# The first sixty microseconds of a Griffin-style block: all of x requested early, the v products ordered by kind, the squares a block later, the forget chain cut in two

## The chip, the cores and the metric

The kernel runs on 1 core of one Trainium2 chip. The metric is device microseconds of one execution. Before the change it is 734.27 us, the median of 3 runs (734.26 to 735.1).

## What is computed

One layer on x of 512 tokens by 1024 channels, batch 1, all in float32:

```python
h = rms_norm(x, norm_mix_g)
cb, cc, cin, q, k, v, f_logit, g_logit = split(h @ w_in)
u = causal_dwconv(cc * cin, conv_mix_w)                 # three taps
y_conv = (cb * u) @ w_out_conv
log_f = log_sigmoid(f_logit + b_f)                      # 8 heads
F = cumsum(log_f)
s = q.k / 8 + F[t] - F[s]   for s <= t                  # 64 channels a head
y_attn = (softmax(s) @ v) @ w_out_attn
g_conv, g_attn = split(sigmoid(g_logit + b_gate))
x = x + (g_conv * y_conv + g_attn * y_attn) @ w_o
h = rms_norm(x, norm_ffn_g)
a, b = split(causal_dwconv(h @ w_up, conv_ffn_w))
x = x + (silu(a) * b) @ w_down
return rms_norm(x, norm_f_g)
```

## The kernel before

Tokens lie along the free dimension, and channels on the partitions, so x is eight tiles `xs0` to `xs7` of 128 x 512. To keep float32 accuracy on the matmul unit, each operand is split into a high and a low part (`xgh`, `xgl` for x times the gain; `wh`, `wl` for a weight), and each product is three matmuls: high by high, low weight by high x, high weight by low x. The factor of the first RMS norm does not depend on the channel, so it is applied after the products.

**Weights.** All weights come through one stream in the order of the list `stream`: eight chunks `v0` to `v7` (one per block of 128 input channels, 520 columns: 512 of v and 8 forget logits), then the q/k chunks `in12`, `in16`, `in13`, `in17`, then the rest. A chunk is fetched into one of four `raw` buffers (`load`, L135, on SyncE's queue, the first on ScalarE's). `split` (L137 to L153) makes `wh` from it on ScalarE (L151; the first on VectorE, L149) and `wl` on VectorE (L152), each with two buffers. So a fetch waits for the `wl` of four chunks before, and a `wh` waits for the matmuls of two chunks before.

**The v stage** (L243 to L296). A loop over the eight blocks `kb`. Block `kb` asks for x two blocks ahead (`load_x`, L248), splits the weight chunk, makes `xgh` (ScalarE, L264) and `xgl` (VectorE, L266), squares x (ScalarE, L273 and L276) and has GpSimd add the square into `ssq` (L277). Then it issues 24 matmuls: for each of four token tiles `t`, each of the three kinds, a product into `pa[t]` (L281: half of v and the forget logits) and one into `pb[t]` (L282: the other half). In block 0 the kinds are the outer loop. In block 7, after token tile 0, `rstd_col` (L183 to L197) multiplies `ssq` by a column of ones into `pc_n` (L189): TensorE waits there for the last addition. VectorE then makes `ms_n`, and GpSimd raises it to the power -0.5 (`rc_n`, L196), which everything behind it needs.

**q, k and the forget gate** (L507 to L530). TensorE projects q0, k0, q1, k1 (`proj`; 48 matmuls each with the chunks `in12`, `in16`, `in13`, `in17`). Between q0 and k0 the forget logits are transposed into `pz`. `forget` (L478 to L494) makes -log(1+exp(-|z|)) on ScalarE (with two table loads), scans it on VectorE (L489), splits the sum into a high part `fh` (ScalarE, L491) and a low one, and writes both to `fr` (L492 to L494). GpSimd's queue copies rows of `fr` into the operands `qb` and `kb` of the scores (L334). `evac_qk` (L336 to L359) scales a projection on VectorE (`t_q`, `t_k`), and writes its high and low parts on ScalarE, GpSimd and VectorE. The accumulator bank of q1 is that of the next projection, `in4` (`p_in`), which may start only when `t_q` of q1 has read it. Attention follows: each unit of scores (L410, L411) lies between halves of further projections.

**What sets the order.** A scheduler places instructions on each engine by their dependencies; `keep` pins an instruction to the written order, and `after_split` puts what is issued under it behind the latest weight split. Each engine works through its own list in order. GpSimd also clears parts of `qb` and `kb` (twelve memsets, L328 to L330), which the scheduler puts between the additions.

Of the kernel before, what the change touches and what calls it, by code (L numbers as in the profile page):

```python
# [24 lines left out]
AHEAD = 3  # L25
NWARM = 8
NPP = 4
# [6 lines left out]
ME, MO = 185, 186  # L34
# [8 lines left out]
def block_kernel(ctx, tc, xT, vecs, wv, win, wmix, wo, wup, wdn, outT):  # L43
# [10 lines left out]
    def keep(ins):  # L54
        return tc.keep_in_program_order(ins)
# [15 lines left out]
    nc.sync.dma_start(vec, vecs)  # L71

    def col(i):
        return vec[:, i : i + 1]
# [56 lines left out]
    def load(upto):  # L131
        for k in range(len(raws), min(upto, len(stream) - 1) + 1):
            nm, src, ncol = stream[k]
            raw = wp.tile([P, RC], F32, tag="raw", name=f"raw_{nm}", bufs=AHEAD + 1)[:, :ncol]
            keep((nc.scalar if k == 0 else nc.sync).dma_start(raw, src))  # L135
            raws.append(raw)

    def split(hl=None):

        k = len(parts)  # L140
        if k == len(stream):
            return
        nm, _, ncol = stream[k]
        load(k + AHEAD)
        hi, lo = hl or [
            wp.tile([P, WC], F32R, tag=f"w{x}", name=f"w{x}_{nm}", bufs=2)[:, WOFF[x] : WOFF[x] + ncol] for x in "hl"
        ]
        if k == 0:
            keep(nc.vector.tensor_copy(hi, raws[k]))  # L149
        else:  # L150
            order["hi"] = nc.scalar.activation(hi, raws[k], AF.Copy).ins  # L151
        order["lo"] = nc.vector.tensor_sub(lo, raws[k], hi.bitcast(F32)).ins  # L152
# [75 lines left out]
    def ct(name):  # L228
        return ap.tile([P, S], F32, tag="ct", name=name, bufs=NCT)
# [22 lines left out]
    load_x(0, halves[0])  # L252
    load(0)
    load_x(0, halves[1])
    load_x(1)
    load(1)
    for kb in range(KB):
        if kb + 2 < KB:
            load_x(kb + 2)
        wh, wl = chunk(f"v{kb}")  # L260
        x = xs[kb]
        cuts = halves if kb == 0 else [slice(0, S)]
        for cs in cuts:
            nc.scalar.activation(xgh[:, kb, cs], x[:, cs], AF.Copy, scale=col(G1 + kb))  # L264
        for cs in cuts:
            ins = nc.vector.scalar_tensor_tensor(  # L266
                xgl[:, kb, cs], x[:, cs], col(G1 + kb), xgh.bitcast(F32)[:, kb, cs],
                op0=ALU.mult, op1=ALU.subtract,
            )
            if kb == 0:  # L270
                keep(ins)
        if kb == 0:
            nc.scalar.activation(ssq, x, AF.Square)  # L273
        else:
            sq = ap.tile([P, S], F32, tag="pp", name=f"sq{kb}", bufs=NPP)
            nc.scalar.activation(sq, x, AF.Square)  # L276
            nc.gpsimd.tensor_add(ssq, ssq, sq)  # L277

        def vmm(t, x, w, start, stop):
            xt = x[:, kb, t * P : (t + 1) * P]  # L280
            keep(nc.tensor.matmul(pa[t][:, :VW], xt, w[:, :VW], start=start, stop=stop))  # L281
            keep(nc.tensor.matmul(  # L282
                pb[t], xt, w[:, VW:], start=start and t % 2 == 0, stop=stop and t % 2 == 1
            ))

        trio = ((xgh, wh), (xgh, wl), (xgl, wh))
        if kb == 0:
# [175 lines left out]
    def run_all(fs):  # L463
        for f in fs:
            f()
# [8 lines left out]
    for t in range(NT):  # L474
        src = pa[t][:, 4 * HD : VW].unsqueeze(1).to_broadcast([P, 4, H])
        nc.vector.tensor_scalar_mul(zn[:, t], src, rc1[:, t : t + 1])

    def forget():  # L478
        n = 4 * H
        bf, me, mo = vec[:n, BF : BF + 1], vec[:n, ME : ME + 1], vec[:n, MO : MO + 1]  # L480
        z, e, o = ct("fz")[:n, :], ct("fe")[:n, :], ct("fo")[:n, :]
# [3 lines left out]
        nc.scalar.activation(tbl, e[:, :1], AF.Exp)  # L485
# [3 lines left out]
        nc.vector.tensor_tensor_scan(e, o, z, 0.0, op0=ALU.mult, op1=ALU.add)  # L489
        hi = ap.tile([n, S], F32R, tag="ct", name="fh", bufs=NCT)  # L490
# [3 lines left out]
        nc.vector.scalar_tensor_tensor(fr, hi.bitcast(F32), me, e, op0=ALU.mult, op1=ALU.add)  # L494
# [347 lines left out]
```

## Time and profile before

| | |
|---|---|
| median of 3 runs | 734.27 us |
| the profiled execution | 734.09 us |
| its span | 732.3 us |
| TensorE (matmul) busy | 717.3 us, 98% of the span |
| VectorE busy | 400.5 us, 55% |
| ScalarE busy | 292.7 us, 40% |
| GpSimd busy | 140.6 us, 19% |
| mean granted TensorE clock | 0.992 |

A row of the timeline has: start, duration, engine, line, operation, what it writes and reads, the shapes, how many, and in brackets how long the engine had been idle before it and what released it. A row with x2 stands for two instructions that follow one another. A row of the windows has: the stretch, its length, then busy time and number of instructions of TensorE (PE), its weight load (PEld), VectorE (DVE), ScalarE (ACT) and GpSimd (POOL), then the granted clock, the busy share of the DMA engines, and GB/s. A row of the waits has: who waited, for whom, the total, how many times, and the longest.

### The profile page before, as it was taken

How to read it: one execution, taken by the hardware profiler on the slowest of the kernel's cores; microseconds unless marked ns; L12 is line 12 of the kernel's file. 1: busy time of each engine (PE TensorE's matmuls, PEld its weight loads, DVE VectorE, ACT ScalarE, POOL GpSimd, SP SyncE). 2: the span in 40 equal slices, each digit the busy share in tenths (PEclk: the TensorE clock that was granted, in tenths of full speed). 3: DMA queues.
4: the chain of work that ended last, by engine and by line, in shares of the span. 5: the costliest groups of instructions: out<-in, count | busy, mean ns of one | idle time of the engine just before them, and what ended most of it. 6: DMA issues, size and time to landing. Idle time of an engine off the chain costs nothing.

```text
span 732.3 us, 14449 instructions
## 1 busy us (share of the span) xinstructions
PE 717.3 (98%) x6220; PEld 715.0 (98%) x6220; DVE 400.5 (55%) x582; ACT 292.7 (40%) x447; POOL 140.6 (19%) x158
## 2 busy tenths in 40 slices
PE   8989999999999999999999999999999999999995
PEld 7889999999999999999999999999999999999995
DVE  6477666765445445454456666666666673223323
ACT  6374545544433332333344344343353442222321
POOL 6515434322001000113311011101101100000100
PEclk9999999999999999999999999999999999999998
DMA  6523222221222332533313332332322423333303
GB/s 211 162 68 104 77 83 60 59 86 58 88 87 87 90 112 88 166 112 129 114 59 116 94 108 87 106 98 87 115 88 87 115 80 102 88 100 100 110 1 115
DMA packets 23296, 71.39 MB, mean 97 GB/s; under 512 B 2976, under 2 KB 5408, under 8 KB 23232
## 3 DMA queue, kind: packets, MB, share of 16 engines
q1 hardware_dynamic: 20848, 66.98, 29.7%
q0 software_dynamic: 1152, 2.17, 1.0%
q10 hardware_dynamic: 1232, 1.32, 0.6%
q8 instruction: 49, 0.80, 0.5%
q14 instruction: 15, 0.12, 0.1%
HBM read 68.29 MB, written 2.10 MB: 96 GB/s over the span
## 4 chain that ended last, share of the span: by engine, by line
PE 92%; DVE 2%; DMA 2%; ACT 1%; issue 1%; SPq 0%; POOLq 0%; POOL 0%; DVEq 0%; ACTq 0%
PE p_up L174 33%; PE pd L174 14%; PE p_in L174 14%; PE p_wo L174 6%; PE p_gb L174 5%; PE p_ga L174 5%; PE yc L174 3%; PE ya L174 3%; PE o L174 2%; DMA xs<-in_xT_dram 2%; PE tp L439 1%; PE pdA L174 1%; PE p_k L174 1%; PE s L410 1%; PE s L411 1%
## 5 line engine op out<-in xcount | busy, mean ns | idle before, releaser
L174 PE MATMUL p_up<-x1h,wh_up 128*128 128x256 f32 x704 | 137.3, 276 | 0.0
L174 PE MATMUL p_up<-x1l,wh_up 128*128 128x256 f32 x704 | 137.1, 276 | 0.0
L174 PE MATMUL p_up<-x1h,wl_up 128*128 128x256 f32 x704 | 137.0, 276 | 0.0
L174 PEld LDWEIGHTS p_up<-x1h,wh_up 128*128 128x128 f32 x704 | 106.1, 188 | 0.0
L174 PEld LDWEIGHTS p_up<-x1l,wh_up 128*128 128x128 f32 x704 | 106.0, 188 | 0.0
L174 PEld LDWEIGHTS p_up<-x1h,wl_up 128*128 128x128 f32 x704 | 105.9, 188 | 0.0
L690 POOL TENSOR_TENSOR fu<-fu,fu 128x512 f32<-128x512 f32 x22 | 28.4, 1293 | 211.2 <-DVE fu L368 198.3
L152 DVE TENSOR_TENSOR wl_in<-raw_in,wh_in 128x1024 fp32r<-128x1024 f32 x36 | 50.3, 1398 | 30.9 <-ACT wh_in L151 30.4
L152 DVE TENSOR_TENSOR wl_up<-raw_up,wh_up 128x1024 fp32r<-128x1024 f32 x44 | 53.7, 1220 | 14.5 <-ACT wh_up L151 14.5
L174 PE MATMUL pd<-gl,wh_dn 128*128 128x256 f32 x308 | 60.1, 276 | 0.0
L174 PE MATMUL pd<-gh,wh_dn 128*128 128x256 f32 x308 | 59.9, 276 | 0.0
L174 PE MATMUL pd<-gh,wl_dn 128*128 128x256 f32 x308 | 59.9, 276 | 0.0
L174 PE MATMUL p_in<-xgh,wh_in 128*128 128x256 f32 x288 | 56.8, 279 | 0.0
L174 PE MATMUL p_in<-xgl,wh_in 128*128 128x256 f32 x288 | 56.4, 277 | 0.0
L174 PE MATMUL p_in<-xgh,wl_in 128*128 128x256 f32 x288 | 56.4, 277 | 0.0
L152 DVE TENSOR_TENSOR wl_dn<-raw_dn,wh_dn 128x1024 fp32r<-128x1024 f32 (+1 forms) x23 | 26.0, 1132 | 54.9 <-ACT wh_dn L151 54.8
L151 ACT ACTIVATE wh_up<-raw_up 128x1024 fp32r<-128x1024 f32 x44 | 46.4, 1055 | 22.3 <-issue 13.4
L151 ACT ACTIVATE wh_in<-raw_in 128x1024 fp32r<-128x1024 f32 x36 | 38.2, 1061 | 42.5 <-PE ya L174 12.7
L151 ACT ACTIVATE wh_dn<-raw_dn 128x1024 fp32r<-128x1024 f32 (+1 forms) x23 | 22.7, 985 | 66.5 <-PE pd L174 66.2
L174 PEld LDWEIGHTS pd<-gl,wh_dn 128*128 128x128 f32 x308 | 46.5, 188 | 0.0
L174 PEld LDWEIGHTS pd<-gh,wh_dn 128*128 128x128 f32 x308 | 46.3, 188 | 0.0
L174 PEld LDWEIGHTS pd<-gh,wl_dn 128*128 128x128 f32 x308 | 46.3, 188 | 0.0
(223 smaller groups left out, 1611.7 us busy)
## 6 DMA issues: line engine op xcount, KB each, us to landing
raw_up<-in_wup_dram SPq DMA_DIRECT2D x44, 512.0 KB, 3.5
raw_in<-in_win_dram SPq DMA_DIRECT2D x36, 512.0 KB, 3.5
raw_dn<-in_wdn_dram SPq DMA_DIRECT2D x16, 512.0 KB, 3.5
raw_mix<-in_wmix_dram SPq DMA_DIRECT2D x8, 512.0 KB, 3.6
raw_wo<-in_wo_dram SPq DMA_DIRECT2D x8, 512.0 KB, 3.9
raw_dn<-in_wdn_dram SPq DMA_DIRECT2D x8, 384.0 KB, 3.3
xr<-in_xT_dram POOLq DMA_DIRECT2D x8, 256.0 KB, 3.8
raw_v<-in_wv_dram SPq DMA_DIRECT2D x7, 260.0 KB, 4.9
```

The source lines that it names most:

```text
L151: order["hi"] = nc.scalar.activation(hi, raws[k], AF.Copy).ins
L152: order["lo"] = nc.vector.tensor_sub(lo, raws[k], hi.bitcast(F32)).ins
L174: keep(nc.tensor.matmul(out[:, cs], w, x[:, cs], start=start and i == 0 and c == 0, stop=stop and i == 2 and c == len(cut) - 1,))
L410: keep(nc.tensor.matmul(s[:, :nn], QT[pr][:, e, qs], KA[pr][:, e, :nn], start=True, stop=False))
L411: keep(nc.tensor.matmul(s[:, :nn], QB[pr % 2][: KR[e], e, qs], KBt[pr % 2][: KR[e], e, :nn], start=False, stop=True))
L439: keep(nc.tensor.transpose(tp[:, ks], pt[:, ks], ident))
L690: nc.gpsimd.tensor_mul(a, a, b)
```

## The change

1. `load_x` for all blocks is issued ahead of the loop, blocks 0 to 3 in turn with their weight chunks, then blocks 4 to 7 together. The table `vecs` is fetched in two parts: columns 0 to 39 first, the other 147 behind all of x.
2. In blocks 0 to 6 the three kinds of v product are the outer loop, and the token tiles the inner one. Block 7 keeps the tiles outside.
3. The square of block `kb` is made in iteration `kb + 1`; the additions of the first squares are written only when the third is there.
4. In block 1 `xgh` is made ahead of the weight split. Splits and parts of x are pinned in the written order.
5. `forget` ends with the scan. What makes `fr` is a function of its own, `forget_rows`, written behind the projection of k0, and so behind the split of the fourth q/k chunk, `in17`; the evacuations of q0 and k0 follow it. The tiles `fz`, `fe`, `fo` use the `pp` buffers in place of `ct`.

```diff
-    load_x(1)
-    load(1)
+    for kb in range(1, AHEAD + 1):
+        load_x(kb)
+        load(kb)
+    for kb in range(AHEAD + 1, KB):
+        load_x(kb)
+    keep(nc.sync.dma_start(vec[:, CM:], vecs[:, CM:]))
+
+    def square_x(kb):
...
+        sq = ap.tile([P, S], F32, tag="pp", name=f"sq{kb}", bufs=NPP)
+        keep(nc.scalar.activation(sq, xs[kb], AF.Square))
+        sqs.append(sq)
+
+        while kb > 2 and sqs:
+            nc.gpsimd.tensor_add(ssq, ssq, sqs.pop(0))
...
     for kb in range(KB):
-        if kb + 2 < KB:
-            load_x(kb + 2)
...
+        if kb:
+            square_x(kb - 1)
+        if kb == KB - 1:
+            square_x(kb)
...
-        if kb == 0:
+        if kb < KB - 1:
             for i, (x, w) in enumerate(trio):
                 for t in range(NT):
-                    vmm(t, x, w, i == 0, False)
+                    vmm(t, x, w, kb == 0 and i == 0, False)
...
     with after_split():
         forget()
+    run_all(proj(16, "k0", st.append, ring(6)))
+    with after_split():
+        forget_rows()
         evac_qk(0, True)(st[0])
-    run_all(proj(16, "k0", evac_qk(0, False), ring(6)))
+        evac_qk(0, False)(st[1])
```

GpSimd's list before, from the first addition into `ssq` to the power that needs the sum (the numbers behind the names tell buffers apart; `sq1` to `sq7` are the squares):

```order
L277 TENSOR_TENSOR ssq1_108<-ssq1_108,sq4_281 128x512
L328 MEMSET qb1_424 4x512
L277 TENSOR_TENSOR ssq1_108<-ssq1_108,sq5_317 128x512
L329 MEMSET qb1_424 64x512
L328 MEMSET kb0_425 4x512
L277 TENSOR_TENSOR ssq1_108<-ssq1_108,sq6_352 128x512
```

GpSimd's list in the changed kernel, the end of the same stretch, where the additions stand one behind another:

```order
L355 MEMSET kb1_427 4x512
L277 TENSOR_TENSOR ssq1_108<-ssq1_108,sq3_278 128x512
L277 TENSOR_TENSOR ssq1_108<-ssq1_108,sq4_315 128x512
L277 TENSOR_TENSOR ssq1_108<-ssq1_108,sq5_350 128x512
L277 TENSOR_TENSOR ssq1_108<-ssq1_108,sq6_385 128x512
L277 TENSOR_TENSOR ssq1_108<-ssq1_108,sq7_388 128x512
L202 TENSOR_TENSOR rc_n1_404<-ms_n1_402,ex_89 128x4
```

Before, one to five memsets stood between two additions. Now eleven of the twelve memsets stand between the first and the third addition, and the last five additions follow one another.

ScalarE's list before, the end of the v stage (`wh_v` the high weights, `xgh` the high x, `sq` the squares):

```order
L151 ACTIVATE wh_v4_275<-raw_v4_163 128x520
L264 ACTIVATE xgh_95<-xs6_271,vec_64 128x512
L276 ACTIVATE sq7_387<-xs6_271 128x512
L151 ACTIVATE wh_v5_311<-raw_v5_200 128x520
L151 ACTIVATE wh_v6_346<-raw_v6_236 128x520
L151 ACTIVATE wh_v7_381<-raw_v7_273 128x520
```

ScalarE's list in the changed kernel, the same place:

```order
L151 ACTIVATE wh_v6_344<-raw_v6_236 128x520
L286 ACTIVATE xgh_95<-xs6_133,vec_64 128x512
L273 ACTIVATE sq5_350<-xs4_130 128x512
L151 ACTIVATE wh_v7_379<-raw_v7_270 128x520
L286 ACTIVATE xgh_95<-xs6_133,vec_64 128x512
L273 ACTIVATE sq6_385<-xs6_133 128x512
L273 ACTIVATE sq7_388<-xs6_133 128x512
```

The last square stood ahead of the high weights of blocks 5, 6 and 7, and now the last two stand behind those of block 7.

VectorE's list before, from the scan of the forget gate to the scaling of q1:

```order
L489 SCALAR_TENSOR_TENSOR fe_557<-fo_558,fz_556 32x512
L341 SCALAR_TENSOR_TENSOR t_q0_572<-p_q0_489,rb_n1_519 128x512
L492 TENSOR_TENSOR fe_557<-fe_557,fh_567 32x512
L493 TENSOR_SCALAR fe_557<-fe_557,vec_64 32x512
L354 TENSOR_TENSOR a_q0_574<-t_q0_572,a_q0_574 64x512
L494 SCALAR_TENSOR_TENSOR fr_451<-fh_567,vec_64,fe_557 32x512
L354 TENSOR_TENSOR a_q0_574<-t_q0_572,a_q0_574 64x512
L152 TENSOR_TENSOR wl_in17_635<-raw_in17_439,wh_in17_634 128x1024
L343 TENSOR_TENSOR t_k0_638<-p_k0_583,rb_n1_519 128x512
```

VectorE's list in the changed kernel, the same place:

```order
L515 SCALAR_TENSOR_TENSOR fe_459<-fo_460,fz_458 32x512
L155 TENSOR_TENSOR wl_in17_620<-raw_in17_440,wh_in17_619 128x1024
L520 TENSOR_TENSOR fe_459<-fe_459,fh_623 32x512
L366 SCALAR_TENSOR_TENSOR t_q0_628<-p_q0_493,rb_n1_523 128x512
L521 TENSOR_SCALAR fe_459<-fe_459,vec_64 32x512
L368 TENSOR_TENSOR t_k0_639<-p_k0_568,rb_n1_523 128x512
L522 SCALAR_TENSOR_TENSOR fr_452<-fh_623,vec_64,fe_459 32x512
L379 TENSOR_TENSOR a_q0_630<-t_q0_628,a_q0_630 64x512 x2
L379 TENSOR_TENSOR kb0_426<-t_k0_639,a_k0_641 64x512 x2
L155 TENSOR_TENSOR wl_in4_702<-raw_in4_446,wh_in4_701 128x1024
L366 SCALAR_TENSOR_TENSOR t_q1_705<-p_q1_650,rb_n1_523 128x512
```

The low weights of `in17`, which stood behind six instructions after the scan, now stand right behind the scan. Those six, and the scaling and splitting of k0, now stand behind them and ahead of `in4` and of the scaling of q1.

More of the change, by code (lines that the diff above doesn't have):

```diff
@@ L70, in block_kernel @@
     vec = cp.tile([P, NV], F32, tag="vec", name="vec")
-    nc.sync.dma_start(vec, vecs)
+    nc.sync.dma_start(vec[:, :CM], vecs[:, :CM])
     def col(i):
@@ L150, in split @@
         else:
-            order["hi"] = nc.scalar.activation(hi, raws[k], AF.Copy).ins
-        order["lo"] = nc.vector.tensor_sub(lo, raws[k], hi.bitcast(F32)).ins
+            ins = nc.scalar.activation(hi, raws[k], AF.Copy)
+            order["hi"] = ins.ins
+            if k < KB:
+                keep(ins)
+        ins = nc.vector.tensor_sub(lo, raws[k], hi.bitcast(F32))
+        order["lo"] = ins.ins
+        if k < KB:
+            keep(ins)
         parts.append((hi, lo))
@@ L254, in block_kernel, with x_hi @@
     load_x(0, halves[1])
[L255 to L256 removed]
+    for kb in range(1, AHEAD + 1):
[5 more added lines that the diff above has]
+    def square_x(kb):
+        if kb == 0:
+            keep(nc.scalar.activation(ssq, xs[kb], AF.Square))
+            return
+        sq = ap.tile([P, S], F32, tag="pp", name=f"sq{kb}", bufs=NPP)
[3 more added lines that the diff above has]
+            nc.gpsimd.tensor_add(ssq, ssq, sqs.pop(0))
+    sqs = []
     for kb in range(KB):
[L258 to L260 removed]
         x = xs[kb]
         cuts = halves if kb == 0 else [slice(0, S)]
+        def x_hi():
+            for cs in cuts:
+                keep(nc.scalar.activation(xgh[:, kb, cs], x[:, cs], AF.Copy, scale=col(G1 + kb)))
+        if kb == 1:
+            x_hi()
+        wh, wl = chunk(f"v{kb}")
+        if kb != 1:
+            x_hi()
         for cs in cuts:
[L264 to L266 removed]
+            keep(nc.vector.scalar_tensor_tensor(
                 xgl[:, kb, cs], x[:, cs], col(G1 + kb), xgh.bitcast(F32)[:, kb, cs],
                 op0=ALU.mult, op1=ALU.subtract,
[L269 to L277 removed]
+            ))
+        if kb:
+            square_x(kb - 1)
+        if kb == KB - 1:
+            square_x(kb)
         def vmm(t, x, w, start, stop):
@@ L476, in block_kernel @@
         nc.vector.tensor_scalar_mul(zn[:, t], src, rc1[:, t : t + 1])
+    n = 4 * H
+    bf, me, mo = vec[:n, BF : BF + 1], vec[:n, ME : ME + 1], vec[:n, MO : MO + 1]
+    z, e, o = (ap.tile([n, S], F32, tag="pp", name=nm, bufs=NPP) for nm in ("fz", "fe", "fo"))
     def forget():
-        n = 4 * H
-        bf, me, mo = vec[:n, BF : BF + 1], vec[:n, ME : ME + 1], vec[:n, MO : MO + 1]
-        z, e, o = ct("fz")[:n, :], ct("fe")[:n, :], ct("fo")[:n, :]
         nc.scalar.activation(e, pz[:n, :], AF.Abs, bias=bf)
@@ L489, in forget, with forget_rows @@
         nc.vector.tensor_tensor_scan(e, o, z, 0.0, op0=ALU.mult, op1=ALU.add)
+    def forget_rows():
         hi = ap.tile([n, S], F32R, tag="ct", name="fh", bufs=NCT)
```

1 line of the change is left out of this document (removed).

## The prediction

> **What bounds the kernel now.** I read the page first, then TensorE's waits, then the windows, then the timelines of single engines.
>
> ```profile
> PE 717.3 (98%) x6220; PEld 715.0 (98%) x6220; DVE 400.5 (55%) x582; ACT 292.7 (40%) x447; POOL 140.6 (19%) x158
> ```
>
> TensorE is busy for 98% of the span. Only 15 us are left to win by waits, and some of those lie at the two ends. The waits of the first 65 us:
>
> ```profile
> PE pa L281 <- DVE wl_v L152: 2.6, 2, 1.7
> PE p_k L174 <- DVE wl_in L152: 2.5, 1, 2.5
> ```
>
> The windows show what a wait costs beyond itself, and where there is nothing to win:
>
> ```profile
> 7.31:10.72 3.41, 1.79 (x12) 1.17 (x10) 2.11 (x3) 3.04 (x6) 2.39 (x3) 1.00 0.98 363
> 10.72:14.13 3.41, 3.41 (x16) 3.41 (x17) 3.41 (x3) 2.49 (x4) 3.41 (x5) 0.53 0.58 180
> 24.37:27.78 3.41, 2.27 (x18) 2.27 (x19) 1.70 (x2) 0.00 (x0) 0.99 (x2) 1.00 0.35 88
> 51.67:55.09 3.42, 1.41 (x13) 1.21 (x11) 3.29 (x5) 0.74 (x1) 1.34 (x4) 1.00 0.00 0
> 55.09:58.50 3.41, 2.97 (x14) 2.97 (x15) 2.66 (x4) 2.32 (x3) 3.19 (x5) 0.53 0.58 153
> 62.00:75.00 13.00, 13.00 (x114) 13.00 (x113) 8.25 (x19) 5.62 (x13) 3.97 (x7) 1.00 0.32 102
> 197.00:360.00 163.00, 163.00 (x1440) 163.00 (x1439) 77.22 (x84) 56.96 (x69) 25.54 (x22) 1.00 0.35 110
> ```
>
> Where TensorE was busy for 1.79 or 1.41 us of 3.41, the granted clock of the next 3.41 us is 0.53; after 2.27 us it stays at 1.00. From 62 us on TensorE doesn't pause. So the time won at 62 us is the time won in all, and two instants carry the sum: `pc_n` (31.86) and the first matmul of `in4` (62.60).
>
> ```profile
> 16.64 0.28 PE L281 MATMUL pa<-wh_v,xgl 128*128 128x264 f32 x1
> ...
> 23.48 0.28 PE L282 MATMUL pb<-wh_v,xgh 128*128 128x256 f32 x1
> ...
> 31.86 0.95 PE L189 MATMUL pc_n<-ones,ssq 128*128 128x1 f32 x8
> ...
> 47.25 0.39 PE L174 MATMUL p_q<-xgh,wh_in 128*128 128x256 f32 x2
> ...
> 52.69 0.39 PE L174 MATMUL p_k<-xgh,wh_in 128*128 128x256 f32 x2
> 55.53 0.80 PE L174 MATMUL p_k<-xgh,wl_in 128*128 128x256 f32 x2 [2.45 <-DVE wl_in L152]
> ...
> 62.60 0.29 PE L174 MATMUL p_in<-xgh,wh_in 128*128 128x256 f32 x1
> ```
>
> Between 16.64 and 23.48 lie 57 steps: 0.12 us a matmul, so 2.88 us a block of 24. A projection at full pace takes 52.69 - 47.25 = 5.44 us. From the start of k1 to `in4`, with two matmuls of scores between, it took 62.60 - 52.69 = 9.91 in place of 5.44 + 0.24, so 4.23 us are lost there. Of these, 1.6 are the halved clock: 23 pairs from 55.53 on need 5.2 us at full pace, and took 62.36 - 55.53 = 6.8.
>
> **Part 1: x early, order by kind.** ScalarE's rows, in the order of time:
>
> ```profile
> 6.81 0.73 ACT L264 ACTIVATE xgh<-xs,vec 128x512 fp32r<-128x512 f32 x1 [1.02 <-DMA xs<-in_xT_dram]
> ...
> 7.96 0.62 ACT L151 ACTIVATE wh_v<-raw_v 128x520 fp32r<-128x520 f32 x1
> ...
> 9.88 0.62 ACT L151 ACTIVATE wh_v<-raw_v 128x520 fp32r<-128x520 f32 x1
> ...
> 14.91 0.64 ACT L151 ACTIVATE wh_v<-raw_v 128x520 fp32r<-128x520 f32 x1 [1.58 <-PE pb L282]
> ...
> 16.07 0.62 ACT L276 ACTIVATE sq<-xs 128x512 f32<-128x512 f32 x1
> ...
> 21.26 0.72 ACT L264 ACTIVATE xgh<-xs,vec 128x512 fp32r<-128x512 f32 x1 [2.01 <-DMA xs<-in_xT_dram]
> ...
> 47.91 0.20 ACT L485 ACTIVATE tbl<-fe 32x1 f32<-32x1 f32 x1
> ...
> 51.34 1.06 ACT L151 ACTIVATE wh_in<-raw_in 128x1024 fp32r<-128x1024 f32 x1
> ```
>
> The last x tile, asked for behind a waiting weight fetch, held ScalarE for 2.01 us up to 21.26. With all of x asked for at the start that goes. In block 1 the square no longer stands between `xgh` and `wh_v`: `wh_v` can start at 7.5, when `xgh` is done, if its data is there, and no later than the 7.96 of before. I take 7.5, and block 1 at 8.1 (bounds 8.1 to 8.6). Ordering by kind lets `wl_v` come 8 matmuls (0.96 us) after the block's start, and `xgl` 16 (1.92 us). TensorE alone then reaches block 7 at 8.1 + 6 x 2.88 = 25.4, and `pc_n` six matmuls later, at 26.1: 5.8 us early, with no halved clock at 10.72. The SyncE queue pays for it: four x tiles and the rest of `vecs`, 1.1 MB, stand ahead of the fourth chunk onward. At the 363 GB/s of the first window that is 3 us. The chunks of blocks 4 to 7 then land about 14 to 16 us, and block 4 starts at 16.7, so I cost it at nothing; a rival takes it up.
>
> **Part 2: the squares later.** This gives part of it back. VectorE's and GpSimd's rows:
>
> ```profile
> 22.02 0.75 DVE L266 SCALAR_TENSOR_TENSOR xgl<-xs,vec,xgh 128x512 fp32r<-128x512 f32 x1 [2.03 <-ACT xgh L264]
> ...
> 23.07 2.39 DVE L152 TENSOR_TENSOR wl_v<-raw_v,wh_v 128x520 fp32r<-128x520 f32 x1 [0.29 <-ACT wh_v L151]
> ...
> 48.20 1.21 DVE L489 TENSOR_TENSOR_SCAN fe<-fo,fz 32x512 f32<-32x512 f32 x1 [0.89 <-ACT tbl L485]
> 49.34 0.65 DVE L341 SCALAR_TENSOR_TENSOR t_q<-p_q,rb_n 128x512 f32<-128x512 f32 x1
> ...
> 54.25 1.23 DVE L152 TENSOR_TENSOR wl_in<-raw_in,wh_in 128x1024 fp32r<-128x1024 f32 x1
> ...
> 56.78 1.71 DVE L354 TENSOR_TENSOR kb<-t_k,a_k 64x512 fp32r<-64x512 f32 x2 [0.70 <-ACT a_k L352]
> ```
>
> ```profile
> L277 POOL TENSOR_TENSOR ssq<-ssq,sq 128x512 f32<-128x512 f32 x7 | 9.9, 1418 | 5.6 <-ACT sq L276 5.4
> ```
>
> ```profile
> 23.15 0.52 POOL L329 MEMSET kb<- 64x512 f32 x1
> 23.64 1.25 POOL L277 TENSOR_TENSOR ssq<-ssq,sq 128x512 f32<-128x512 f32 x1
> ...
> 53.81 1.27 POOL L334 DMA_DIRECT2D qb<-fr  x2 [2.08 <-DVE fr L494]
> ...
> 56.19 1.76 POOL L353 TENSOR_SCALAR a_k<-t_k 64x512 fp32r<-64x512 f32 x2
> ```
>
> An addition takes 1.25 us when free. One beside the `wl_v` at 23.07 stretched that from about 0.7 to 2.39: the two exclude one another. The `xgl` at 22.02 took its 0.75 us beside memsets, so these cost GpSimd's own time only.
>
> Now the sum. `wh_v` of block 2 starts between 8.5 (behind `wh_v` of block 1 and a square) and the 9.88 of before, say 9.2; the first square ends 1.16 + 0.62 later (14.91 to 16.07, and its own length), at 11.0. GpSimd does the first addition to 12.4, five memsets at 0.52 to 15.0, the second behind a `wl_v` from 15.5 to 16.7, six memsets to 19.8. Then five additions are left, and the two-input instructions of blocks 6 and 7 come in turn with them: 5 x 1.25 + 2 x (0.69 + 0.75) = 9.1, so `ssq` is there at 28.8 in place of the 26.1 where TensorE wants it. Lower bound: the last squares follow `wh_v` of block 7, which follows block 5's end (22.5), so they end at 24.9, and the last addition at 26.9. Upper bound, with each addition at the 1.42 of the group row: 30.0. I take 28.8; `pc_n` comes 31.86 - 28.8 = 3.1 us early.
>
> TensorE would be idle for about 2.7 of the 3.4 us from 25.4 to 28.8: less busy than the two windows that were followed by 0.53. So I expect a halved clock behind it. It cost 1.6 us at k1; part of it falls into the wait, and I take 1.2 (bounds 0 and 1.6).
>
> **Part 3: the forget chain split.** From `pc_n` on, the power, the evacuations and the chain follow as before, so I keep the clock of before. `wh_in` of `in17` goes behind the table of 47.91, to 49.17, `wl_in` behind the scan at 49.34 to 50.6; TensorE wants it at 52.9. The loss of 4.23 goes. What is late next: behind `wl_in` VectorE has five instructions at about 0.7 (as `t_q`), two pairs at 1.71, `wl_in` of `in4` at 1.23 and `t_q` of q1 at 0.65: 50.6 + 3.5 + 3.4 + 1.2 + 0.65 = 59.3, less 0.8, since each starts some 0.07 before the record of the one ahead ends (the scan's ends at 49.41, and `t_q` starts at 49.34): 58.5. That `t_q` frees the bank of `in4`, which TensorE wants at 52.69 + 5.44 + 0.24 = 58.37. A wait of 0.1 to 0.9, say 0.4. The score before it wants `kb`: GpSimd has `qb` and `a_k` (1.76 a pair) behind `t_k`, to 55.4, then the copies.
>
> ```profile
> DMA to landing us min/median/max: 1.6/2.5/3.7
> ```
>
> The first copy into `kb` starts at 55.4 + 1.27 = 56.7 and lands at 58.3 if it takes 1.6, and 60.4 at 3.7; no weight fetch runs beside it, so I take 1.6, inside the 0.4. After that the projections of attention give VectorE time to catch up (8.25 of 13 us busy after 62 before).
>
> From `pc_n` to `in4`: before 30.74. Now 30.74 - 4.23 + 0.4 = 26.9 without the halved clock; with it TensorE comes 1.2 later, the 0.4 is covered, 27.7.
>
> **Sum.** 28.8 + 27.7 = 56.5 against 62.60: 6.1 us. The profiled execution took 734.09 (0.18 below the median), so 728.0.
>
> **Rivals.**
>
> *The sum is in time.* If additions get ahead of VectorE, `pc_n` is at 26.9, no clock falls, and `in4` starts at 26.9 + 26.9 = 53.8: 8.8 us, 725.3. For it: the group's 1.42 contains waits that may shrink. Against: GpSimd has at least 6.2 us of additions left at 19.8, beside VectorE's 2.9. Chance 0.18.
>
> *The clock stays.* [...] Chance 0.20.
>
> *The weights come late.* If the chunks of blocks 4 and on move at the 180 GB/s of the second window, 1.1 MB takes 6 us, block 4 waits some 2.3 us, and the end moves by as much: 730.3. Against: the busiest window had 363. Chance 0.14.
>
> *The fourth weights are still late*, from a wait on ScalarE or its fetch that I don't see. Then only part 1 is won: 3.1 us, 731.0. Chance 0.07.
>
> *Slower: GpSimd and VectorE take turns throughout*, memsets too. The `wl_v` at 23.07 was held 0.57 us before the addition's record began, beside a memset. Then from 11.0 on all is one row: 7 x 1.25 + 11 x 0.52 + 12 x 0.7 = 22.9, `pc_n` at 33.9, two halved windows of 1.6, and `in4` at 33.9 + 26.9 + 3.2 = 64.0: 735.5 at least. It decides from `pc_n` at about 33 on. Against: the 0.75 us `xgl` beside memsets. [...] Chance 0.04.
>
> **How the numbers follow.** My case has 0.37, and its bounds reach from 26.9 + 26.6 to 30.0 + 28.1 for `in4`, which is 725.0 to 729.6. The range reaches from the first rival's 725.3 to the late weights' 730.3, with 0.1 and 0.2 of margin, 725.2 to 730.5; outside are the last two rivals, 0.11, and a tail. A measurement can tell about 0.2%, 1.5 us. All cases but the last are faster, 0.96; half of the third rival's chance I give to no change, since late weights may join it, and a quarter of the slower one: faster 0.93, same 0.04, slower 0.03.
>
> **What would show it.** Right: blocks 1 to 6 without a wait over 0.3 us; a wait of TensorE on `ssq` or on `xgl` of block 7 of about 2.7 us, `pc_n` near 28.8, a granted clock near 0.5 behind it; no wait at k1, a short one at the first score or at `in4`. Wrong: a wait in blocks 4 to 7 for a fetch; `pc_n` before 27 or after 30; a wait on `wl_in` at k1; pauses of TensorE in attention, which would give time back.

## The result, and the profile after

The changed kernel takes 728.13 us, the median of 4 runs (727.26 to 728.9), beside 734.26 us for the kernel before in the same comparison (4 runs, 734.08 to 735.1). The ratio is 0.9914, 95% interval 0.9897 to 0.9931. The forecast was 728.0, in a range of 725.2 to 730.5.

The kernel before is less steady than those four runs suggest. Beside the experiments below it ran 66 times more: 65 of these lie between 729.36 and 735.56 us, with a median near 732.2 (one run of 746.5, at a mean clock of 0.942, is left aside). The changed kernel stayed at 727.3 to 728.9 in 11 runs. In the later comparison the ratio is 0.9941 (0.992 to 0.9962). So the gain is 6.1 us against the runs that the forecast started from, and about 4 against an ordinary one.

The profiled execution after took 728.21 us, with a span of 726.4. The busy time on the page, and TensorE's waits in the first 65 us:

```profile
PE 716.0 (99%) x6220; PEld 714.3 (98%) x6220; DVE 396.9 (55%) x582; ACT 293.0 (40%) x447; POOL 140.9 (19%) x158
```

```profile
PE pc_n L195 <- POOL ssq L277: 1.5, 1, 1.5
...
PE pa L306 <- ACT xgh L286: 0.2, 1, 0.2
```

(The row left out is the wait of the first `ones`, ahead of the v stage, in both kernels.) The waits for `wl_v` in the v stage and for `wl_in` at k1 are gone. One new wait is there, for the sum of squares. TensorE's rows at the two instants that carried the sum, and between them two rows at the ends of the stretch at half pace:

```profile
28.20 1.05 PE L195 MATMUL pc_n<-ones,ssq 128*128 128x1 f32 x8 [1.51 <-POOL ssq L277]
...
29.92 0.34 PE L306 MATMUL pa<-wh_v,xgh 128*128 128x264 f32 x1
...
33.30 0.47 PE L180 MATMUL p_q<-xgl,wh_in 128*128 128x256 f32 x2
...
56.09 0.28 PE L435 MATMUL s<-a_k,a_q 128*128 128x256 f32 x1
56.21 0.30 PE L436 MATMUL s<-kb,qb 68*128 68x256 f32 x1
56.37 0.47 PE L180 MATMUL p_in<-xgh,wh_in 128*128 128x256 f32 x2
```

`pc_n` starts at 28.20 (31.86 before, 28.8 forecast), and `in4` at 56.37 (62.60 before, 56.5 forecast). That is 6.23 us. The span is shorter by 5.9: 0.3 to 0.4 is given back at the very end, where the last matmuls ran at a lower clock this time (0.58 granted in the 1.2 us around them, against 1.00 before). The first row is of the kernel before, the second of the changed one:

```profile
725.55 0.71 PE L203 MATMUL pb_n<-ident,rc_n 128*128 128x128 f32 x4 [1.02 <-POOL rc_n L196]
```

```profile
719.34 1.11 PE L209 MATMUL pb_n<-ident,rc_n 128*128 128x128 f32 x4 [1.03 <-POOL rc_n L202]
```

The windows of the changed kernel around the wait:

```profile
26.50:29.90 3.40, 1.89 (x16) 1.70 (x15) 0.61 (x2) 0.57 (x1) 1.94 (x3) 1.00 0.42 145
29.90:33.30 3.40, 3.40 (x19) 3.40 (x18) 2.09 (x8) 1.48 (x4) 2.06 (x2) 0.52 0.47 146
```

TensorE was busy for 1.89 of 3.40 us, and behind that the clock was halved for about 3.4 us, from 29.9 to 33.3 (0.52 granted, and some 0.22 us a matmul in place of 0.12).

What ends the wait is seen on GpSimd, ScalarE and VectorE, in this order:

```profile
18.98 0.52 POOL L355 MEMSET kb<- 4x512 f32 x1
19.47 4.36 POOL L277 TENSOR_TENSOR ssq<-ssq,sq 128x512 f32<-128x512 f32 x3
25.05 3.10 POOL L277 TENSOR_TENSOR ssq<-ssq,sq 128x512 f32<-128x512 f32 x2 [1.22 <-ACT sq L273]
```

```profile
23.13 0.64 ACT L151 ACTIVATE wh_v<-raw_v 128x520 fp32r<-128x520 f32 x1 [1.10 <-PE pb L307]
23.68 0.71 ACT L286 ACTIVATE xgh<-xs,vec 128x512 fp32r<-128x512 f32 x1
24.29 1.13 ACT L273 ACTIVATE sq<-xs 128x512 f32<-128x512 f32 x2
```

```profile
18.66 0.75 DVE L295 SCALAR_TENSOR_TENSOR xgl<-xs,vec,xgh 128x512 fp32r<-128x512 f32 x1
...
24.91 0.74 DVE L295 SCALAR_TENSOR_TENSOR xgl<-xs,vec,xgh 128x512 fp32r<-128x512 f32 x1
```

(The `xgl` at 18.66 is used further below.) GpSimd was through its backlog at 23.83 and stood idle for 1.22 us, until ScalarE had the last two squares ready behind `wh_v` and `xgh` of block 7. The last two additions then took 3.10 in place of 2 x 1.25, partly beside the `xgl` at 24.91: that one ended at 25.65, and 25.65 + 2 x 1.25 is 28.15, where the sum ended. So the sum was late for another reason than the one forecast.

### The profile page after: what moved, and what is told of

The parts are those of the page before. It is cut to its first block, busy times and chain, and to the rows that moved or that the text cites. A ratio compares the mean times of both kernels' runs of the same rounds, so it can differ in the third digit from the quotient of the medians.

```text
span 726.4 us, 14453 instructions
## 1 busy us (share of the span) xinstructions
PE 716.0 (99%) x6220; PEld 714.3 (98%) x6220; DVE 396.9 (55%) x582; ACT 293.0 (40%) x447; POOL 140.9 (19%) x158
## 3 DMA queue, kind: packets, MB, share of 16 engines
q1 hardware_dynamic: 20992, 66.98, 29.5%
## 4 chain that ended last, share of the span: by engine, by line
PE 97%; issue 1%; POOL 1%; DMA 0%; DVE 0%; ACT 0%; POOLq 0%; DVEq 0%; SPq 0%; ACTq 0%
PE p_up L180 33%; PE pd L180 14%; PE p_in L180 14%; PE p_wo L180 6%; PE p_gb L180 5%; PE p_ga L180 5%; PE yc L180 3%; PE ya L180 3%; PE o L180 2%; PE p_q L180 2%; PE pa L306 2%; PE p_k L180 2%; PE pb L307 1%; PE tp L464 1%; PE pdA L180 1%
## 5 line engine op out<-in xcount | busy, mean ns | idle before, releaser
L721 POOL TENSOR_TENSOR fu<-fu,fu 128x512 f32<-128x512 f32 x22 | 28.4, 1291 | 211.2 <-DVE fu L393 198.3
L180 PE MATMUL p_in<-xgl,wh_in 128*128 128x256 f32 x288 | 56.5, 277 | 0.0
L180 PE MATMUL p_in<-xgh,wl_in 128*128 128x256 f32 x288 | 56.4, 277 | 0.0
```

The lines of the kernel that those rows point to most:

```text
L180: keep(nc.tensor.matmul(out[:, cs], w, x[:, cs], start=start and i == 0 and c == 0, stop=stop and i == 2 and c == len(cut) - 1,))
L721: nc.gpsimd.tensor_mul(a, a, b)
```

## The experiments

All were timed beside the kernel before. The text at the head of each result was written ahead of the run. Theory 1 is that of the prediction. Theory 2 came from the trace after: the end of the sum is set by the order on ScalarE and not by a backlog on GpSimd.

| kernel | median, us | range (runs) | ratio to before |
|---|---|---|---|
| the change, again | 728.02 | 727.32 to 728.36 (7) | 0.9941 (0.992 to 0.9962) |
| forget chain whole | 729.94 | 729.31 to 730.97 (12) | 0.9969 (0.9953 to 0.9985) |
| before, with the forget chain split | 730.52 | 727.24 to 731.27 (12) | 0.9957 (0.9936 to 0.9977) |
| squares in their own block | 726.40 | 725.75 to 727.31 (6) | 0.992 (0.9893 to 0.9947) |
| memsets early | 727.30 | 726.88 to 727.5 (6) | 0.9931 (0.9907 to 0.9955) |
| wait filled with matmuls | 727.14 | 726.82 to 727.6 (6) | 0.9933 (0.9911 to 0.9955) |
| all squares a block ahead, memsets early | 727.32 | 726.15 to 729.28 (8) | 0.9937 (0.9915 to 0.996) |
| last squares ahead, memsets early | 726.20 | 725.44 to 726.85 (6) | 0.9922 (0.9895 to 0.9948) |
| x asked for late | 728.11 | 727.1 to 730.32 (11) | 0.9951 (0.9934 to 0.9968) |
| token tiles outside | 728.17 | 727.62 to 728.98 (8) | 0.9948 (0.9928 to 0.9967) |
| x late and token tiles outside | 727.51 | 726.84 to 728.12 (6) | 0.9935 (0.9911 to 0.9958) |

### The two halves of the change

The change without its last part:

```diff
     with after_split():
         forget()
-    run_all(proj(16, "k0", st.append, ring(6)))
-    with after_split():
         forget_rows()
         evac_qk(0, True)(st[0])
-        evac_qk(0, False)(st[1])
+    run_all(proj(16, "k0", evac_qk(0, False), ring(6)))
```

> The change with its last part undone: the forget chain is again in one piece, ahead of the fourth weights' split. Theory of the prediction (the parts add up, and the loss at k1 belongs to the chain alone): pc_n stays at 28.2, TensorE waits for wl_in at k1 again. From pc_n to in4 between 29.1 (the halved clock behind pc_n hides part of the wait, and no second halved clock follows) and 30.7 us as before, so in4 at 57.3 to 58.9 and the whole at 729.1 to 730.6. Rival (the early v stage alone makes the fourth weights early enough): no wait at k1, in4 at 56.4, 728.1.

729.94 us. The wait at k1 is there, shorter than the 2.5 of before, because a halved clock behind `pc_n` (at 27.78, behind a wait of 1.36; matmuls 0.22 us apart in place of 0.12 from 29.6 to 32.9) had made TensorE late:

```profile
PE p_k L180 <- DVE wl_in L155: 1.7, 1, 1.7
```

No halved clock followed the wait at k1 in the profiled execution (1.00 granted from 52.0 to 55.4), and `in4` started at 57.90, inside the 57.3 to 58.9 of theory 1. So the early v stage alone does not make the fourth weights early.

The kernel before with the last part alone:

```diff
     with after_split():
         forget()
+    run_all(proj(16, "k0", st.append, ring(6)))
+    with after_split():
+        forget_rows()
         evac_qk(0, True)(st[0])
-    run_all(proj(16, "k0", evac_qk(0, False), ring(6)))
+        evac_qk(0, False)(st[1])
```

(`forget` is cut behind the scan, and its three tiles are in `pp`, as in the change.)

> The kernel before with the last part of the change alone: the forget chain split behind the fourth weights. Theory of the prediction: pc_n stays at 31.9, no wait of TensorE at k1 and no halved clock behind it, 4.2 us less loss, and 0.1 to 0.9 us given back at the first score or at in4, now that no halved clock behind pc_n covers it: in4 at 58.5 to 59.3, 730.0 to 730.8. Rival (the wait only moves to the score or to the bank of in4): in4 at 60.5 or later, 732 or more.

730.52 us, as theory 1 had it. The profiled execution has no wait at k1, the old waits in the v stage, and a new one at the first score:

```profile
PE pa L281 <- DVE wl_v L152: 3.1, 5, 0.9
...
PE s L411 <- DMA kb<-fr: 0.5, 1, 0.5
```

`pc_n` starts at 31.62 and `in4` at 58.93, 27.31 later. Against the common median of before, 732.81, the two halves gain 2.9 and 2.3 us. They add up, within the spread of before, to what the whole gains. Four of the twelve runs took 727.2 to 727.8 and the others 730.5 to 731.3; no profile shows one of the four.

### What the sum of squares waits for

Squares in their own block, right behind `xgl`:

```diff
-        if kb:
-            square_x(kb - 1)
-        if kb == KB - 1:
-            square_x(kb)
+        square_x(kb)
```

> The change with each block's squares in its own block, right behind xgl, so that ScalarE takes only the last block's squares after the last wh_v and xgh. Theory drawn from the trace of after (the wait of 1.5 us at pc_n ends when ScalarE lets GpSimd have the last two squares): GpSimd's idle time of 1.2 us before the last two additions goes, ssq is there at 26.6 to 27.2, TensorE waits under 0.5 us, no halved clock behind pc_n, in4 at 53.8 to 54.6, 725.5 to 726.5. Rival (the sum of the prediction: GpSimd is behind through memsets and turns with VectorE, whenever the squares come): ssq at 28 or later, 728 as after. Second rival: the squares ahead of the next wh_v delay early blocks on ScalarE by 0.6 us each, and TensorE waits there.

726.40 us. The wait for `ssq` is gone from TensorE's waits, and the clock is not halved (1.00 granted in every stretch from 18 to 38 us):

```profile
25.93 1.51 POOL L277 TENSOR_TENSOR ssq<-ssq,sq 128x512 f32<-128x512 f32 x1 [1.47 <-ACT sq L273]
```

```profile
27.49 1.05 PE L195 MATMUL pc_n<-ones,ssq 128*128 128x1 f32 x8
```

Only one addition is left behind ScalarE's last square. `in4` starts at 54.89, above the 53.8 to 54.6 expected, with the sum of squares at 27.4 in place of 26.6 to 27.2. The second rival did not occur as written: no block waited for ScalarE. But the first addition now comes at 9.03, beside `xgl` of block 1 (the two that met additions later here, at 20.91 and 23.23, took 1.79 and 1.78 us in place of 0.75); TensorE waited 0.28 us for it, at 10.93, and reached `pc_n` at 27.49, 0.8 later than the 26.69 at which the change wanted it.

The memsets of `qb` and `kb` ahead of the v stage:

```diff
+    for t in (*QB, *KBt):
+        tf = t.bitcast(F32)
+        keep(nc.gpsimd.memset(tf[HD : HD + 4, 0, :], 1.0))
+        keep(nc.gpsimd.memset(tf[:HD, 1, :], 0.0))
+        keep(nc.gpsimd.memset(tf[:4, 1, :], 1.0))
     ssq = cp.tile([P, S], F32, tag="ssq", name="ssq1")
...
-    for t in (*QB, *KBt):
...
```

> The change with the memsets of qb and kb placed ahead of the v stage on GpSimd, so that the first addition no longer stands between them. Theory drawn from the trace of after (the end of the sum is set by ScalarE's order): the first five additions come some 4 to 5 us earlier, the last two stay behind the last squares, GpSimd's idle time before them grows, ssq at 27.7 to 28.2, 727.5 to 728.5, as after. Rival (the backlog on GpSimd, as the prediction summed it): ssq at 26.9, no halved clock, 725.3 to 726.3.

727.30 us, nearer to theory 2. The backlog is gone, GpSimd waits for ScalarE ahead of each addition, and the pair at the end still comes last:

```profile
21.66 1.28 POOL L286 TENSOR_TENSOR ssq<-ssq,sq 128x512 f32<-128x512 f32 x1 [1.59 <-ACT sq L282]
24.54 2.63 POOL L286 TENSOR_TENSOR ssq<-ssq,sq 128x512 f32<-128x512 f32 x2 [1.59 <-ACT sq L282]
```

```profile
27.22 1.05 PE L195 MATMUL pc_n<-ones,ssq 128*128 128x1 f32 x8 [1.04 <-POOL ssq L286]
```

It is 1 us earlier than in the change's first execution: 0.5 from an earlier start of block 1 in this execution (8.02 against 8.51), and 0.5 from the pair, which took 2.63 in place of 3.10, since VectorE was nearly through with `xgl` of block 7 by then (it ended at 24.66, and the pair began at 24.54). The backlog that the prediction summed is worth no more than the second 0.5. The wait is shorter, 1.04 us, and the clock was halved behind it all the same:

```profile
25.79:29.19 3.40, 2.36 (x20) 2.15 (x19) 0.88 (x2) 0.77 (x1) 1.94 (x3) 0.99 0.33 129
29.19:32.60 3.41, 3.41 (x18) 3.41 (x17) 2.02 (x8) 1.83 (x4) 1.79 (x2) 0.51 0.45 151
```

TensorE was busy for 2.36 us ahead of it, more than the 2.27 of the kernel before (24.37 to 27.78) that was followed by no halved clock. So the busy share that the profile shows, by which the prediction judged, does not settle alone whether the clock falls.

### The clock, and the spread of the kernel before

The kernel before, once more, unchanged:

> The kernel before once more, for a second profiled execution, since its runs here spread from 729.5 to 735.6 us. [...] Rival: the waits themselves differ, since the last x tile lands at another time: pc_n moves by over 1 us from 31.86 at the same clock.

734.88 us, again at the upper end of the spread. `pc_n` stands where it stood, and at k1 the wait of 2.5 and the halved clock are there again (0.75 granted in the 6.8 us from 54.4 on, with pairs 0.43 us apart in place of 0.23 from 56.4 to 59.4):

```profile
PE p_k L174 <- DVE wl_in L152: 2.5, 1, 2.5
```

```profile
32.03 0.95 PE L189 MATMUL pc_n<-ones,ssq 128*128 128x1 f32 x8
```

The halved clock of the v stage (10.72 to 14.13 in the first profile) is not there (the matmuls from 10.8 to 13.2 are 0.12 us apart): one halved stretch fewer, and yet no gain, 734.88 against 734.09 us. TensorE waited longer for the same operands instead, 3.6 us in place of 2.6:

```profile
PE pa L281 <- DVE wl_v L152: 3.6, 5, 0.9
```

The change, once more, unchanged:

> The changed kernel once more, beside the same runs of the kernel before. Theory: it has one wait with a halved clock behind it, and this comes in nearly every execution, so its runs spread less than those of before, 727.2 to 729, median 728. Rival: it spreads as much as before, over 3 us.

728.02 us, and a spread of 1 us, as the theory had it. But the clock did not follow it. This execution has the same wait, and no halved clock behind it (1.00 granted from 28.4 to 35.2):

```profile
28.50 1.05 PE L195 MATMUL pc_n<-ones,ssq 128*128 128x1 f32 x8 [1.50 <-POOL ssq L277]
...
54.87 0.28 PE L435 MATMUL s<-a_k,a_q 128*128 128x256 f32 x1
55.70 0.35 PE L436 MATMUL s<-kb,qb 68*128 68x256 f32 x1 [0.55 <-DMA kb<-fr]
55.91 0.47 PE L180 MATMUL p_in<-xgh,wh_in 128*128 128x256 f32 x2
```

The two executions of one kernel give both prices, and the runs above and below agree: from `pc_n` to the first score it is 27.9 us in the two more that have a halved clock and no wait at k1 (memsets early, 0.51 granted; x asked for late, 0.22 us a matmul from 30.9 on), and 26.2 to 26.4 in the six that have none. Here it is 26.37 us, and 56.09 - 28.20 = 27.89 in the first profile of the change: the halved clock costs 1.52. From the first score to `in4` it is 1.04 here and 0.28 there, and two scores at full pace take 0.24: the wait for `kb` costs 0.80 when nothing covers it. What is left between the two is 0.76 of 728. Waits of 1.51 and 1.50 us were followed, the one by 3.4 us at 0.52 and the other by 1.00 throughout; what decides between the two is not shown.

Six more matmuls of `ones` by `ones`, into a bank that nothing reads, in the time of the wait:

```diff
                 if (kb, t) == (KB - 1, 0):
+                    for _ in range(6):
+                        keep(nc.tensor.matmul(warm[:, :P], ones, ones, start=True, stop=True))
```

> The change with six more matmuls of ones by ones into a bank that nobody reads, between the last block's first token tile and pc_n: 1.3 to 1.6 us of work in the 1.5 us in which TensorE waits for ssq; pc_n comes no earlier. Theory of the prediction (the halved clock behind the stall costs 1.2 us, and covers a short wait at the first score): pc_n at 28.2, no halved clock behind it, TensorE is 1.2 us earlier at the first score, which then waits 0.5 us for kb as it does in the run with the squares in their own block; in4 at 55.4 to 55.8, 727.2 to 727.6. Rival (the clock doesn't follow the stall): the halved stretch stays, 728.1.

727.14 us, below the change and just under the 727.2 to 727.6 expected. The clock stays up (0.12 us a matmul from 29.74 on); `pc_n` is late by the wait for `xgl` and the filling:

```profile
27.04 0.39 PE L306 MATMUL pa<-wh_v,xgl 128*128 128x264 f32 x1 [1.03 <-DVE xgl L295]
...
27.39 1.50 PE L322 MATMUL warm<-ones 128*128 128x128 f32 x12
28.73 0.95 PE L195 MATMUL pc_n<-ones,ssq 128*128 128x1 f32 x8
...
55.47 0.47 PE L180 MATMUL p_in<-xgh,wh_in 128*128 128x256 f32 x2
```

```profile
20.03 8.09 POOL L277 TENSOR_TENSOR ssq<-ssq,sq 128x512 f32<-128x512 f32 x5
...
29.96 1.03 POOL L202 TENSOR_TENSOR rc_n<-ms_n,ex 128x4 f32<-128x4 f32 x1 [1.84 <-DVE ms_n L200]
```

Two things were not expected. GpSimd did the last five additions in one row here, to 28.12, beside VectorE (8.09 us in place of 5 x 1.25, while `xgl`, `wl_v` and `xgl` took 1.77 to 1.80 each), and TensorE waited 1.03 us for `xgl` of block 7: the course that the prediction had written down, ending within 0.1 us of the other one. And from `pc_n` to `in4` it took 26.74, not 27.4, with hardly a wait for `kb`: the power `rc_n` took 1.03 us, where it had taken 1.95 beside a `wl_in` of VectorE, and the score that reads `kb` started 26.52 us behind `pc_n` (55.25), in place of 27.20. That is another order and not the filling: here VectorE's list has this `wl_in` ahead of `ms_n` (26.91, right behind the last `xgl`), and in the change behind it (29.37).

So the 0.9 us between the medians are not the price of the clock alone. The mean clock of the single runs is a hint at its share: of the change's eleven runs six show 0.992 or 0.993 and took 728.06 to 728.9 us, five show 0.995 to 0.997 and took 727.26 to 728.02. All six with the filled wait show 0.995 to 0.997. Since the clock at the end of the span (0.58 against 1.00, above) moves this mean too, it counts no executions exactly.

### The squares further ahead

All squares a block ahead of their products, with the memsets early:

```diff
-        if kb:
-            square_x(kb - 1)
-        if kb == KB - 1:
-            square_x(kb)
+        if kb == 0:
+            square_x(0)
+        if kb + 1 < KB:
+            square_x(kb + 1)
```

> The change with both undone on which the sum of squares waits: each block's squares a block ahead of its products, and the memsets of qb and kb ahead of the v stage. Theory drawn from the traces so far (only ScalarE's order and the additions behind it hold up pc_n): the last addition is done before 25, pc_n starts when TensorE gets there, 26.1 to 26.6, no halved clock; from there 27.4 to in4 with a wait of 0.5 us for kb at the first score, as in the run with the squares in their own block: in4 at 53.5 to 54.0, 725.0 to 725.6. Rival: the squares ahead delay wh_v and xgh on ScalarE in blocks 1 and 2 and TensorE waits there by 0.6 us or more: 725.6 to 727.

727.32 us. `pc_n` has no wait, but comes at 28.58, and the time is lost in blocks 1 and 2, though not where the rival put it. VectorE's, GpSimd's and TensorE's rows:

```profile
9.39 2.41 DVE L304 SCALAR_TENSOR_TENSOR xgl<-xs,vec,xgh 128x512 fp32r<-128x512 f32 x1
11.73 1.78 DVE L155 TENSOR_TENSOR wl_v<-raw_v,wh_v 128x520 fp32r<-128x520 f32 x1
```

```profile
11.69 2.99 POOL L286 TENSOR_TENSOR ssq<-ssq,sq 128x512 f32<-128x512 f32 x2
```

```profile
11.86 0.39 PE L315 MATMUL pa<-wh_v,xgl 128*128 128x264 f32 x1 [0.68 <-DVE xgl L304]
```

The additions come early, where VectorE has no time to spare, and TensorE waits 0.68 and 0.27 us for `xgl`. Block 1 itself started at 9.09 in place of 8.51, without a wait: in this execution block 0 began 0.27 later and ran longer at half pace (0.22 us a matmul, to 7.17 in place of 6.05), which need not come from the edit.

The last squares alone ahead, blocks 1 to 4 as in the change, the memsets early:

```diff
-        if kb:
+        if 0 < kb < KB - 2:
             square_x(kb - 1)
-        if kb == KB - 1:
+        if kb == KB - 3:
             square_x(kb)
+        if kb == KB - 2:
+            square_x(kb)
+            square_x(kb + 1)
```

> The change with the memsets of qb and kb ahead of the v stage, and the last squares alone brought forward: block 5 takes the squares of x tiles 4 and 5, block 6 those of 6 and 7, block 7 none; blocks 1 to 4 stay as in the change. Theory (the sum waits for ScalarE's last two squares, and squares ahead of blocks 1 and 2 are what held up the run with all squares a block ahead): no wait in blocks 1 to 6, the last addition ends at 24.5 to 25.2, pc_n at 26.2 to 26.7 without a wait and without a halved clock; then a wait of 0.5 to 0.6 us for kb at the first score; in4 at 53.6 to 54.1, 725.1 to 725.7. Rival: the additions of 20 to 25 us meet wl_v and xgl of blocks 6 and 7 on VectorE, each pair takes its turns, and TensorE waits about 1 us for xgl of block 7: 726.0 to 726.6.

726.20 us, the fastest of all by median, though 0.5 above the range expected; the squares in their own block, at 726.40, are not told apart from it. All six runs (at most 726.85) lie below all eleven of the change (at least 727.26).

```profile
27.01 0.95 PE L195 MATMUL pc_n<-ones,ssq 128*128 128x1 f32 x8
...
54.10 0.36 PE L440 MATMUL s<-kb,qb 68*128 68x256 f32 x1 [0.54 <-DMA kb<-fr]
54.31 0.47 PE L180 MATMUL p_in<-xgh,wh_in 128*128 128x256 f32 x2
```

The time lies in the rival's range, but its wait for `xgl` is 0.16 us in place of about 1. `pc_n` to `in4` is 27.30, with the wait for `kb` in it.

### What took the waits out of blocks 1 to 7

x asked for as before:

```diff
-    for kb in range(1, AHEAD + 1):
-        load_x(kb)
-        load(kb)
-    for kb in range(AHEAD + 1, KB):
-        load_x(kb)
+    load_x(1)
+    load(1)
...
+        if kb + 2 < KB:
+            load_x(kb + 2)
         wh, wl = chunk(f"v{kb}")
```

> The change with the requests for x as before: each tile two blocks ahead, on SyncE behind fetches that wait for a buffer. Theory of the prediction, taken one step further (before, the last xgh was done at 21.9, while the new order of products wants it only at 25.3, so early x matters only through block 1 and the squares): no wait of TensorE for xgh, 727.5 to 728.8. Rival (early x is what makes pc_n early): a wait for xgh or wh_v of 1 to 3 us in blocks 3 to 7, 729 to 731.

728.11 us, and no wait for x after block 0. `pc_n` is where it was in the change:

```profile
28.54 1.05 PE L195 MATMUL pc_n<-ones,ssq 128*128 128x1 f32 x8 [1.49 <-POOL ssq L274]
```

The order of the products as before:

```diff
-        if kb < KB - 1:
+        if kb == 0:
             for i, (x, w) in enumerate(trio):
```

> The change with the order of the products of blocks 1 to 6 as before: token tile by token tile, so that wl_v is wanted 0.24 us after a block's start and xgl 0.48. Theory of the prediction (the order by kind is what hides a VectorE that takes turns with GpSimd): waits for wl_v and xgl come back wherever an addition runs beside them, 1.5 to 3 us in all, partly taken out of the 1.5 us wait at pc_n, since that ends when ScalarE and GpSimd are done: 728.2 to 730. Rival (the order by kind does nothing, early x and late squares do): no waits over 0.3 us in blocks 1 to 6, 728.0.

728.17 us. The waits come back, but small:

```profile
PE pc_n L195 <- POOL ssq L277: 0.5, 1, 0.5
PE pa L306 <- DVE xgl L295: 0.4, 2, 0.2
...
PE pa L306 <- DVE wl_v L155: 0.2, 1, 0.2
```

They come partly out of the wait at `pc_n`, as expected: it falls from 1.5 to 0.5, and the clock stays up (0.12 us a matmul from 30.15 on).

Both of these undone together:

> The change with both the requests for x and the order of the products of blocks 1 to 6 as before: what is left of its first two parts is the order on ScalarE and VectorE (wh_v, xgh, squares a block late; wl_v and xgl of one block in turn). Theory (that order is what took the waits for wl_v away, since before VectorE did the xgl of the block after ahead of wl_v; early x and the order by kind each added little): pc_n at 28.5 to 29.5, short waits of 0.2 to 0.5 us for wl_v and xgl, 728 to 729. Rival (early x and the order by kind stand in for each other, and one of them is needed): waits of 2 us or more in blocks 1 to 7, pc_n at 30.5 to 32, 730 to 731.3, as the kernel before with the split forget chain alone.

727.51 us, half a microsecond below the 728 to 729 expected, and `pc_n` at 28.64, inside the 28.5 to 29.5:

```profile
PE pc_n L195 <- POOL ssq L274: 0.6, 1, 0.6
PE s L435 <- DMA kb<-fr: 0.5, 1, 0.5
PE pa L305 <- DVE xgl L294: 0.4, 2, 0.2
```

So neither early x nor the order by kind is needed. What stays of the first part in this kernel is the order that the pins give to ScalarE and VectorE, and the table `vecs` fetched in two parts. VectorE's list, to the left of the kernel before and to the right of this one, from the low weights of block 1 on:

```
wl_v1                         wl_v1
xgl of block 1                xgl of block 1
xgl of block 2                wl_v2
wl_v2                         xgl of block 2
xgl of block 3                wl_v3
xgl of block 4                xgl of block 3
wl_v3                         wl_v4
```

Before, VectorE made `xgl` of later blocks ahead of the `wl_v` that TensorE wanted next. The run with squares in their own block undid the other thing that stays here, their lag, and had no wait for `wl_v` either. No run undid all three at once, and none put the order of the kernel before back into the change, so it is not shown that the order alone is enough; it is what the other runs leave.

## Why the prediction held, step by step

**Block 1 and the v stage: right in time, wrong in cause.** Block 1 started at 8.51, inside the 8.1 to 8.6; the blocks followed at full pace, and `pc_n` was wanted at 28.20 - 1.51 = 26.69, in place of 26.1. The prediction put this down to early x and to the order by kind. With both undone the time is 727.5. What it counted only for block 1's `wh_v`, the new order on the engines that make the operands, is what remains to explain the other blocks too; no run isolates it.

**Late weights: did not occur.** All of x was asked for ahead, and blocks 4 to 7 show no wait for a fetch. ScalarE started their `wh_v` at 14.49, 17.37, 20.25 and 23.13, each behind a wait of 1.10 or 1.11 us for TensorE and none for the chunk; the chunk of block 4 was there by 14.49, early in the 14 to 16 of the prediction.

**The sum of squares: nearly right, by another path.** 28.8 was forecast and 28.15 measured (25.05 + 3.10). The forecast summed a backlog on GpSimd (its terms, 19.8 + 9.1, give 28.9). In the profiled execution GpSimd was idle for 1.22 us, and ScalarE's last two squares set the end. The prediction had this path as its lower bound, 26.9, but too short: the squares ended at 25.42 in place of 24.9, the first of the two additions started at 25.05, and the pair took 3.10 beside `xgl`. One execution of five additions in a row, ending at 28.12, shows that the summed path exists too. TensorE was idle 1.5 us, not 2.7, since it came later and the sum earlier.

**The halved clock: followed in one execution, not in another.** The forecast's case and its rival (the clock stays) were both measured, in two executions of one kernel. Against the rival's 0.20 the mean clocks above hint at five executions in eleven; what decides between the two no run shows. The cost is 1.52 in place of 1.2. From `pc_n` to `in4` the two cases differ by 0.76 us, where the prediction had 0.8. Its ground was weaker than it looked: it took the busy share of 3.41 us for the sign, and the memsets-early run has a halved clock behind 2.36 us.

**The loss at k1: gone, as forecast.** The work that takes its place is the wait for `kb`, named in the prediction beside that for the bank of `in4`; it cost 0.80 uncovered, in place of 0.4, and 0.04 behind a halved clock. So the mechanism was right and two sizes were off: `pc_n` to `in4` is 28.17 with the halved clock (27.7 forecast) and 27.41 without (26.9 forecast).

**The sum.** 28.20 + 28.17 = 56.37, against 28.8 + 27.7 = 56.5. Two errors, -0.6 in the first half and +0.5 in the second, nearly cancel, so the closeness of the total is in part luck. With what was lost at the end of the span it came to 728.21 for a forecast of 728.0. (In the chances, "half of the third rival's" fits the 0.04 for no change only if the rival of the fourth weights, 0.07, is meant.)

**The slower rival: excluded.** Memsets and VectorE did not take turns: the `xgl` at 18.66 lasted 0.75 us although a memset ran beside it (18.98 to 19.50), as long as the one at 9.03 with GpSimd idle; the one at 22.61, beside an addition, took 1.77.

**What the prediction left out** is the spread of the kernel before. Its base was one execution at 734.09, like the three runs known then, and ordinary executions take about 732.2. What makes them differ stays open: the three profiles with the old v stage have `pc_n` at 31.6 to 32.0, and both profiles of before have the wait and the halved clock at k1, so no profile shows an execution from the lower end of the spread.

## What to carry to other kernels

Where several engines prepare operands, look first at what stands ahead of the operand that is wanted next in each engine's own list (here the early fetch and the new order of products could both go, 727.51 us against 728.02), and price an early fetch or a new order of products only behind that. Where work is moved back to get it out of the way, look for the reduction that hangs on its last piece; here that was two squares, made behind the last block's operands. With the memsets early, bringing only the last squares forward won 1.8 us; bringing all of them forward won 1.1 less, in part at least since the additions then met VectorE in the first blocks. Each block's squares in their own block won 1.6, with the memsets left where they were. A forecast in microseconds needs the spread of its base as well as its own sum.

## What the runs showed of the hardware

- A GpSimd instruction of 128 x 4 elements, the power `rc_n`, took 1.95 us beside a `wl_in` of VectorE (in the change) and 1.03 when that was done (with the wait filled): on a chain that everything waits for, 0.9 us are lost to an operand that, in the changed kernel, is done at 30.60 and first read at 32.87.
- The same wait of 1.5 us was followed by 3.4 us at half clock (0.52 granted) in one execution and by none (1.00) in another, and a wait of 1.04 us, with TensorE busy for 2.36 of 3.40 us, was followed by it too. From `pc_n` to the first score the halved clock cost 1.5 to 1.7 us (27.9 against 26.2 to 26.4), and about half of that (0.76 of 1.52 in the change) came out of a later wait.
- VectorE's `xgl` took 0.75 us alone or beside memsets, and mostly 1.77 to 2.41 us beside GpSimd's additions; the one at 24.91 in the change took 0.74, and there the pair of additions from 25.05 on took 3.10 in place of 2.5.
